# Five pairs of split weight tiles, four loaded ones, and seven-product sums that grow in two PSUM tiles

## The chip, the cores and the metric

The kernel runs on one NeuronCore of one Trainium2 chip. Times are device microseconds of one execution of the whole program; a time is the median of a few executions, and beside it stands the profile of one execution, whose span is a little shorter than its time. The engines are named as in the profile: PE (matrix multiplies; PEld are its weight loads), DVE (vector engine), ACT (scalar engine), POOL (GpSimd) and SP (issues DMAs).

## The reference

One decoder layer over 1024 prompt tokens and 8 sequences of 4 decode tokens, 1056 tokens in all, in float32. The parts that the change touches are the two FFN products into the hidden width of 2816:

```python
def _layer(x, p, ...):
    ...
    x = x + _rms(mix, n_mix_post)
    f = _rms(x, n_ffn_pre)
    f = (jax.nn.silu(f @ w_gate) * (f @ w_up)) @ w_down
    x = x + _rms(f, n_ffn_post)
    x = x + jax.nn.sigmoid(x @ w_ple_gate) * (p @ w_ple)
```

Before it stand an input projection, a causal pooling mixer, sliding-window attention with sinks, and an output projection.

## The kernel before

**Tiles.** Tokens lie along the free dimension in three groups of 352 (groups 0, 1 and 2), channels along the 128 partitions. Each float32 product is made of three reduced-precision ones: an operand is split into a rounded part and the rest (`split`, L163: ScalarE casts the rounded part, L164, VectorE subtracts it, L165), and `gemm` (L278) issues high x high, high x low and low x high for each 128 channels. A product over 512 channels is 12 matmuls of 128x352, one over 1024 channels 24.

**The FFN.** The hidden width is cut into 22 chunks of 128, two to a slab. `WALK` lists the order of slabs: entries 0 to 4 do slabs 0 to 4 for group 2 alone, entries 5 to 10 do slabs 5 to 10 for all three groups, entries 11 to 15 do slabs 0 to 4 for groups 0 and 1. `gate_up` does one chunk of one entry. Group 2 is multiplied directly (`direct`, 24 matmuls for gate and 24 for up). Groups 0 and 1, gate and up together, are a 2x2 block product that is done with seven 512-channel products instead of eight (`product`, 12 matmuls each): two use quarters of the gate tile (with `f7["B11"]`, `f7["B21"]`), one a quarter of the up tile (`T4`), and four use sums and differences of weight quarters, S1 to S4 (with `T1`, `T2`, `T3`, `B22`). The products are added to one another in SBUF on VectorE, read once each from PSUM (`add`, L1024).

**The weight sums.** `w_sums` (L980) makes S1 to S4 in place in the two loaded tiles: four POOL operations (L990), which can only begin when both loaded tiles have been split (the subtraction reads them), and then two casts (`sh`) and two subtractions (`sl`) of 128x1024.

**The down products.** `downs` of an entry are issued inside the first chunk of the next one (`pending`): 8 output tiles per group of 6 matmuls each, every one read from PSUM by VectorE and added to `os_` (L1087). The first of them that read a chunk's result wait for `hid_put` (L977), a cast on ScalarE and a subtraction on VectorE.

**Pools and order.** Split weights lie in 2 x `W_PAIRS` tiles, loaded ones in `W_RAW` tiles. PSUM has 8 banks, one tile each (`bank`). `need` makes the weight items up to `LOOK` = 4 ahead in the program. The order on PE is pinned to the program's order; on ScalarE, VectorE and POOL a scheduler sets it when the program is built, and each engine then runs its instructions in that order. VectorE and ScalarE work of the norms (`ple_steps`, `ffn_steps`) is dealt out between products by `turn`.

Of the kernel before, what the change touches and what calls it, by code (L numbers as in the profile page):

```python
# [12 lines left out]
AF = mybir.ActivationFunctionType  # L13
ALU = mybir.AluOpType
# [33 lines left out]
UEXT = PST + DSEQ  # L48
ULEN = UPRE + SEQ + NDEC * UEXT

W_PAIRS = 4
W_RAW = 3


WARM = 8
# [6 lines left out]
def trunk_kernel(  # L62
# [31 lines left out]
    nc = tc.nc  # L94
    te, ve, se, ge = nc.tensor, nc.vector, nc.scalar, nc.gpsimd
# [10 lines left out]
    def nm(s):  # L106
        cnt[0] += 1
        return f"{s}{cnt[0]}"
# [15 lines left out]
    def mm(*args, **kw):  # L124

        ins = te.matmul(*args, **kw)  # L126
# [63 lines left out]

    def weights(j, ahead=W_PAIRS - 1):
        for i in range(j, j + (0 if lazy[0] else ahead) + 1):
# [71 lines left out]
    def need(k, ahead=LOOK):  # L264

        for i in range(len(made), min(k + ahead + 1, len(ITEMS))):
            kind, js = ITEMS[i]
            if kind == "direct":
                w_split(js[0])
                made[i] = pairs[js[0]]  # L270
            else:
                made[i] = w_sums(*(raws[ITEMS[j][1][0]] for j in js))
            for kind, js in ITEMS[i + 1 : i + 3]:
                if kind == "direct":
                    w_load(js[0])
        return made[k]

    def gemm(ps, ops, start=True, stop=True):  # L278

        last = len(ops) - 1  # L280
        for i, (wh, wl, xh, xl) in enumerate(ops):
            mm(ps, wh, xh, start=start and i == 0, stop=False)
            mm(ps, wh, xl, start=False, stop=False)
            mm(ps, wl, xh, start=False, stop=stop and i == last)

    def ops8(w, xs):

# [147 lines left out]
    n = 4 * NDEC * PST  # L435
# [145 lines left out]
    for c in range(4):  # L581
        n = NDEC * DSEQ
# [356 lines left out]
    f7 = {}  # L939
# [37 lines left out]
    def hid_put(g, slot, ht):  # L977
        split(new_hid[g][:, slot, :], new_hid[g][:, SLAB + slot, :], ht)
# [20 lines left out]
    def ops4(w, x):  # L999

        return [(w[0][:, k, :], w[1][:, k, :], x[0][:, k, :], x[1][:, k, :]) for k in range(4)]

    def quarter(w, h):
        return tuple(t[:, 4 * h : 4 * h + 4, :] for t in w)

    def gate_up(items, slot, gs, pending):

        ig, iu, is_ = items
        n = N

        def product(w, x):
            ps = bank()
            gemm(ps[:, :n], ops4(w, x))
            turn(12)
            return ps[:, :n]

        def direct(w):
            ps = bank()
            gemm(ps[:, :n], ops8(w, fs[2]))
            turn(24)  # L1020
            return ps[:, :n]

        def add(out, a, ps):
            ve.tensor_tensor(out, a, ps, op=ALU.add)  # L1024

        wg = need(ig)
        if 0 in gs:
            p1 = tmp(n, "p1")
            se.copy(p1, product(quarter(wg, 0), f7["B11"]))
        if 2 in gs:  # L1030
            sl = tmp(n, "sl")
            se.activation(sl, direct(wg), AF.Silu)
        if 0 in gs:
            c11 = tmp(n, "c11")
            add(c11, p1, product(quarter(wg, 1), f7["B21"]))
            se.activation(c11, c11, AF.Silu)
        if pending and 0 in gs:
            pending()
        wu = need(iu)
        if 2 in gs:  # L1040
            ve.tensor_tensor(sl, sl, direct(wu), op=ALU.mult)
        for g in gs:
            if slot == 0:
                new_hid[g] = half(g, F32R, "hid")
        if 2 in gs:
            hid_put(2, slot, sl)
        if pending and 0 not in gs:
            pending()
        if 0 not in gs:
            return  # L1050
# [7 lines left out]
        if 2 in gs:  # L1058
# [8 lines left out]
        se.activation(p1, p1, AF.Silu)  # L1067
        ve.tensor_tensor(u3, u3, p1, op=ALU.mult)
        hid_put(1, slot, u3)

    os_ = [None] * G

# [204 lines left out]
```

## Time and profile before

| | before |
|---|---|
| median of 3 runs | 1118.25 us (1117.61 to 1118.88) |
| the profiled execution | 1118.37 us, its span 1116.6 us |
| PE busy | 1106.5 us (99%), 7171 matmuls |
| DVE busy | 748.3 us (67%) |
| ACT busy | 440.0 us (39%) |
| POOL busy | 179.4 us (16%) |
| mean granted PE clock | 0.998 |

Busy time is a share of the whole span. PE's matmuls are pipelined: one of 128x352 is shown with some 0.32 us, and they start some 0.16 us apart. The idle time named beside a group of instructions is that of its engine just before it, with what ended it. The entries of `WALK` that carry all three groups lie at about 400 to 770 us of the span, entries 11 to 15 at about 770 to 985 us.

### The profile page before, as it was taken

What the parts mean: (1) busy time and instruction counts of PE and PEld (TensorE: products, weight loads), DVE (VectorE), ACT (ScalarE), POOL (GpSimd) and SP (SyncE); (2) the same over time, 40 slices, a digit from 0 to 9 for tenths busy, and PEclk for the clock granted to TensorE, in tenths of its full rate; (3) what the DMA queues carried; (4) which work ended last, traced back from release to release, by engine and by line L of the source; (5) the groups of instructions that cost most, each with busy time, mean ns of one, the idle gap of its engine ahead of it and who ended that gap; (6) DMA issues with size and microseconds to landing.
All of it is one profiled execution on the core that took longest, in us unless ns stands there. A gap on an engine that the chain in (4) does not pass through costs nothing.

```text
span 1116.6 us, 17703 instructions
## 1 busy us (share of the span) xinstructions
PE 1106.5 (99%) x7171; PEld 1089.6 (98%) x7171; DVE 748.3 (67%) x1241; ACT 440.0 (39%) x779; POOL 179.4 (16%) x152
## 2 busy tenths in 40 slices
PE   8999999999999999999999999999999999999998
PEld 8999988899999999999999999999999999999998
DVE  6667478886979955255564555547887877789532
ACT  8323276664645523331222313123424334365220
POOL 0045032200000131011111102112132123100000
PEclk9999999999999999999999999999999999999999
DMA  8121311542543212121120202122112222336211
GB/s 289 56 71 38 122 43 38 194 157 85 203 166 129 99 38 76 39 76 39 38 60 17 78 36 76 38 100 79 57 58 83 70 76 80 124 133 222 85 58 39
DMA packets 35217, 99.54 MB, mean 89 GB/s; under 512 B 4132, under 2 KB 14660, under 8 KB 35136
## 3 DMA queue, kind: packets, MB, share of 16 engines
q1 hardware_dynamic: 33808, 96.65, 25.5%
q10 hardware_dynamic: 1328, 1.77, 0.5%
q8 instruction: 56, 0.92, 0.3%
q14 instruction: 25, 0.20, 0.1%
HBM read 88.30 MB, written 10.11 MB: 88 GB/s over the span
## 4 chain that ended last, share of the span: by engine, by line
PE 93%; DVE 3%; DMA 1%; issue 1%; POOL 1%; ACT 1%; SPq 0%; DVEq 0%; POOLq 0%
PE b L126 92%; PE b L120 1%; DMA xr<-in_x_dram 1%; DVE wl L165 1%; POOL wr L990 0%; SPq L342 0%; DVE h L368 0%; DVE o L1115 0%; DVE x L1119 0%; DVE mx L628 0%; DVE a L736 0%; DVE p L1024 0%; DVE hid L165 0%; ACT h L366 0%; ACT xr L377 0%
## 5 line engine op out<-in xcount | busy, mean ns | idle before, releaser
L126 PE MATMUL b<-fh,wh 128*128 128x352 f32 x808 | 260.7, 323 | 0.0
L126 PE MATMUL b<-fh,wl 128*128 128x352 f32 x808 | 259.3, 321 | 0.0
L126 PE MATMUL b<-fl,wh 128*128 128x352 f32 x808 | 259.0, 321 | 0.0
L126 PE MATMUL b<-hid,wh 128*128 128x352 f32 x1056 | 252.5, 322 | 1.8 <-DVE o L1115 1.2
L164 ACT CAST wh<-wr 128x1024 fp32r<-128x1024 f32 (+1 forms) x139 | 143.0, 1031 | 248.9 <-PE b L126 205.6
L165 DVE TENSOR_TENSOR wl<-wr,wh 128x1024 fp32r<-128x1024 f32 (+1 forms) x139 | 170.5, 1229 | 57.9 <-ACT wh L164 53.9
L126 PEld LDWEIGHTS b<-hid,wh 128*128 128x128 f32 x1056 | 182.3, 188 | 2.6 <-issue 1.5
L126 PE MATMUL b<-hid,wl 128*128 128x352 f32 x528 | 169.0, 320 | 0.0
L990 POOL TENSOR_TENSOR wr<-wr 128x512 f32<-128x512 f32 x44 | 63.4, 1441 | 623.0 <-DVE wl L165 621.3
L126 PEld LDWEIGHTS b<-fl,wh 128*128 128x128 f32 x808 | 151.9, 188 | 0.0
L126 PEld LDWEIGHTS b<-fh,wl 128*128 128x128 f32 x808 | 151.8, 188 | 0.0
L126 PEld LDWEIGHTS b<-fh,wh 128*128 128x128 f32 x808 | 151.6, 188 | 0.0
L1087 DVE TENSOR_TENSOR o<-o,b 128x352 f32<-128x352 f32 x240 | 114.9, 516 | 29.3 <-PE b L126 29.3
L126 PE MATMUL b<-fh,sh 128*128 128x352 f32 x352 | 113.6, 323 | 0.0
L126 PE MATMUL b<-fl,sh 128*128 128x352 f32 x352 | 112.7, 320 | 0.0
L126 PE MATMUL b<-fh,sl 128*128 128x352 f32 x352 | 112.7, 320 | 0.0
L126 PE MATMUL b<-h,wh 128*128 128x352 f32 x480 | 105.5, 325 | 0.9 <-ACT h L366 0.6
L165 DVE TENSOR_TENSOR sl<-wr,sh 128x1024 fp32r<-128x1024 f32 x44 | 53.8, 1222 | 75.5 <-ACT sh L164 75.5
L126 PEld LDWEIGHTS b<-hid,wl 128*128 128x128 f32 x528 | 98.9, 187 | 0.0
L164 ACT CAST sh<-wr 128x1024 fp32r<-128x1024 f32 x44 | 45.7, 1047 | 130.9 <-POOL wr L990 91.2
L126 PEld LDWEIGHTS b<-h,wh 128*128 128x128 f32 x480 | 81.9, 189 | 2.2 <-DVE h L368 1.2
L126 PE MATMUL b<-h,wl 128*128 128x352 f32 x240 | 66.3, 326 | 0.0
(150 smaller groups left out, 1591.0 us busy)
## 6 DMA issues: line engine op xcount, KB each, us to landing
wr<-in_w_gu_dram SPq DMA_DIRECT2D x64, 512.0 KB, 3.3
wr<-in_w_dn_dram SPq DMA_DIRECT2D x32, 512.0 KB, 3.3
wr<-in_w_pg_dram SPq DMA_DIRECT2D x14, 512.0 KB, 3.6
x<-in_x_dram SPq DMA_DIRECT2D x6, 704.0 KB, 7.1
x1d<-x SPq DMA_DIRECT2D x6, 704.0 KB, 3.5
x<-x1d SPq DMA_DIRECT2D x6, 704.0 KB, 6.7
out_y_dram<-yo SPq DMA_DIRECT2D x24, 176.0 KB, 1.9
wr<-in_w_out_b_dram SPq DMA_DIRECT2D x8, 512.0 KB, 3.3
```

Source lines behind the costliest of these rows:

```text
L120: ins = te.transpose(out, src, ident)
L126: ins = te.matmul(*args, **kw)
L164: fix(se.copy(hi, src))
L165: fix(ve.tensor_tensor(lo, src, hi.bitcast(F32), op=ALU.subtract))
L990: ge.tensor_tensor(out, a, b, op=op)
L1087: ve.tensor_tensor(o, o, v, op=ALU.add)
```

## The change

- `W_PAIRS` goes from 4 to 5 and `W_RAW` from 3 to 4: ten tiles of split weights instead of eight, four loaded ones instead of three. Room for them comes from a smaller scratch area that the program reserves for DMAs.
- Two PSUM tiles, `row` and `col`, take several of the seven products, one added to the other by PE (`start=False`, `onto=True`). `row` grows by B11, S2, S3 and, where group 2 takes part, T4; `col` by S1 and S4.
- Between the products a partial sum is read out. ScalarE copies it (`copied`: after B11, after S2, after S1 and, in the chunks without group 2, after S3), VectorE adds the rest. A product onto `row` or `col` may not begin before the copy of what it held.
- The order of products within a chunk changes. With group 2 it was B11, gate for group 2, B21, (downs), up for group 2, S2, S3, T4, S1, S4, and is now B11, gate for group 2, B21, (downs), S2, S1, S3, S4, up for group 2, T4. Without group 2 it was B11, B21, (downs), T4, S2, S3, S1, S4, and is now B11, B21, (downs), T4, S2, S1, S3, S4.

```diff
-W_PAIRS = 4
-W_RAW = 3
+W_PAIRS = 5
+W_RAW = 4
...
-    def gemm(ps, ops, start=True, stop=True):
+    def gemm(ps, ops, start=True, stop=True, onto=False):
...
-            mm(ps, wh, xh, start=start and i == 0, stop=False)
+            mm(ps, wh, xh, start=start and i == 0, stop=False, skip_group_check=onto)
...
-        def product(w, x):
-            ps = bank()
-            gemm(ps[:, :n], ops4(w, x))
+        def product(w, x, ps=None, start=True):
+            onto = ps is not None
+            ps = ps if onto else bank()
+            gemm(ps[:, :n], ops4(w, x), start, onto=onto)
             turn(12)
             return ps[:, :n]
...
-        def add(out, a, ps):
+        def add(a, ps, s):
+            out = tmp(n, s)
             ve.tensor_tensor(out, a, ps, op=ALU.add)
+            return out
+
+        def copied(ps, s):
+            out = tmp(n, s)
+            se.copy(out, ps)
+            return out
...
         if 0 in gs:
-            p1 = tmp(n, "p1")
-            se.copy(p1, product(quarter(wg, 0), f7["B11"]))
-        if 2 in gs:
+            row = bank()
+            p1 = copied(product(quarter(wg, 0), f7["B11"], row), "p1")
+        if third:
             sl = tmp(n, "sl")
             se.activation(sl, direct(wg), AF.Silu)
         if 0 in gs:
-            c11 = tmp(n, "c11")
-            add(c11, p1, product(quarter(wg, 1), f7["B21"]))
+            c11 = add(p1, product(quarter(wg, 1), f7["B21"]), "c11")
             se.activation(c11, c11, AF.Silu)
...
-        if 2 not in gs:
+        s = need(is_)
+        col = bank()
+        if not third:
             p4 = product(quarter(wu, 1), f7["T4"])
-        s = need(is_)
-        add(p1, p1, product(s["S2"], f7["T2"]))
-        u3 = tmp(n, "u3")
-        add(u3, p1, product(s["S3"], f7["T3"]))
-        c21 = tmp(n, "c21")
-        if 2 in gs:
-            p4 = product(quarter(wu, 1), f7["T4"])
-        add(c21, u3, p4)
-        ve.tensor_tensor(c21, c21, c11, op=ALU.mult)
-        hid_put(0, slot, c21)
-        p5 = product(s["S1"], f7["T1"])
-        add(u3, u3, p5)
-        add(p1, p1, p5)
-        add(p1, p1, product(s["S4"], f7["B22"]))
-        se.activation(p1, p1, AF.Silu)
-        ve.tensor_tensor(u3, u3, p1, op=ALU.mult)
-        hid_put(1, slot, u3)
+        u2 = copied(product(s["S2"], f7["T2"], row, False), "u2")
+        p5 = copied(product(s["S1"], f7["T1"], col), "p5")
+        p7 = product(s["S3"], f7["T3"], row, False)
+        if not third:
+            u3 = copied(p7, "u3")
+        u1 = add(p5, p7, "u1")
+        if not third:
+            ve.tensor_tensor(u3, u3, p4, op=ALU.add)
+            ve.tensor_tensor(u3, u3, c11, op=ALU.mult)
+            hid_put(0, slot, u3)
+        c12 = add(u2, product(s["S4"], f7["B22"], col, False), "c12")
+        se.activation(c12, c12, AF.Silu)
+        ve.tensor_tensor(u1, u1, c12, op=ALU.mult)
+        hid_put(1, slot, u1)
+        if third:
+            third_up()
+            ve.tensor_tensor(c11, c11, product(quarter(wu, 1), f7["T4"], row, False), op=ALU.mult)
+            hid_put(0, slot, c11)
...
-    nc = _bacc.Bacc("TRN2", target_bir_lowering=False, num_devices=1)
+    nc = _bacc.Bacc("TRN2", target_bir_lowering=False, num_devices=1, dynamic_dma_scratch_size=1024)
```

On PE the rows are as many as before (6129), and they differ only inside `gate_up`. On ACT they go from 667 to 721, on DVE from 1206 to 1122. Three places on ACT carry the prediction. Names end in a number that tells buffers of one kind apart: `wr` is a loaded weight tile, `wh` the rounded part of a direct tile, `sh` that of a summed one, `b` a PSUM tile, `hid` a hidden operand; `p`, `u`, `c` and `sl` are the sums of a chunk.

**First place**: ACT in the first chunk of entry 11 (slab 0, groups 0 and 1), from the casts of the weights of the second chunk on. Before:

```order
L164 CAST wh_7589<-wr_7462 128x1024
L164 CAST wh_7700<-wr_7556 128x1024
L304 ACT_TABLE_LOAD
L304 ACTIVATE sd_7874<-b_7869,c_86 88x4
L164 CAST sh_7818<-wr_7462 128x1024
L164 CAST hid_7828<-c_7900 128x352
L164 CAST sh_7822<-wr_7556 128x1024
L1029 COPY p_7944<-b_7945 128x352
```

Changed:

```order
L164 CAST wh_7652<-wr_7508 128x1024
L305 ACT_TABLE_LOAD
L305 ACTIVATE sd_7826<-b_7821,c_86 88x4
L164 CAST sh_7770<-wr_7390 128x1024
L1033 COPY u_7836<-b_7510 128x352
L1033 COPY p_7850<-b_7788 128x352
L164 CAST sh_7774<-wr_7508 128x1024
L1033 COPY u_7864<-b_7510 128x352
```

`b_7510` is this chunk's `row`, `b_7788` its `col`. The cast `sh_7770` is of the second chunk's sums, and the copy of `row` after S2 (`u_7836`) stands behind it. `wr_7508` is the second chunk's up tile: `wh_7652` takes over the buffer of the down weights that entry 11's `pending` uses last.

**Second place**: ACT in the first chunk of entry 12. Before:

```order
L164 CAST wh_8118<-wr_7996 128x1024
L164 CAST wh_8186<-wr_8083 128x1024
L164 CAST hid_8270<-c_8320 128x352
L164 CAST sh_8260<-wr_7996 128x1024
L164 CAST sh_8264<-wr_8083 128x1024
L1067 ACTIVATE p_8085<-p_8085 128x352
```

Changed:

```order
L164 CAST wh_8070<-wr_7935 128x1024
L164 CAST wh_8138<-wr_8035 128x1024
L1033 COPY u_8256<-b_8037 128x352
L164 CAST sh_8212<-wr_7935 128x1024
L1033 COPY p_8270<-b_8230 128x352
L164 CAST sh_8216<-wr_8035 128x1024
L1033 COPY u_8284<-b_8037 128x352
```

Here the copy of `row` after S2 stands ahead of the summed cast, and the copy of `col` after S1 (`p_8270`) behind it. Entries 13, 14 and 15 have the same sequence. In the first chunks of entries 5 to 10 both copies stand ahead of the summed casts.

**Third place**: ACT from the end of entry 11's second chunk into entry 12. Before:

```order
L164 CAST wh_7975<-wr_7847 128x1024
L164 CAST wh_7992<-wr_7942 128x1024
L1067 ACTIVATE p_7944<-p_7944 128x352
L1029 COPY p_8085<-b_8086 128x352
L164 CAST hid_7829<-u_8018 128x352
L164 CAST sh_8075<-wr_7704 128x1024
L1036 ACTIVATE c_8100<-c_8100 128x352
L164 CAST sh_8079<-wr_7942 128x1024
```

Changed:

```order
L164 CAST wh_7931<-wr_7894 128x1024
L1033 COPY u_7997<-b_7896 128x352
L164 CAST sh_8027<-wr_7656 128x1024
L1033 COPY p_8050<-b_8037 128x352
L1078 ACTIVATE c_8017<-c_8017 128x352
L164 CAST sh_8031<-wr_7894 128x1024
L164 CAST hid_7780<-u_7997 128x352
L164 CAST hid_7781<-u_7999 128x352
```

Both casts of hidden operands stood ahead of the summed casts or, for the first of the chunk, further up; now both stand behind `sh_8027` and `sh_8031`. On DVE the subtraction that belongs to `sh_8027` likewise stands ahead of those that belong to `hid_7780` and `hid_7781`. `wh_7931`, the next up tile, takes over a buffer that S3 of this second chunk uses last. In entries 13 to 15 the `hid` casts stand ahead of the `sh` casts.

More of the change, by code (lines that the diff above doesn't have):

```diff
@@ L276, in need @@
         return made[k]
-    def gemm(ps, ops, start=True, stop=True):
+    def gemm(ps, ops, start=True, stop=True, onto=False):
         last = len(ops) - 1
         for i, (wh, wl, xh, xl) in enumerate(ops):
-            mm(ps, wh, xh, start=start and i == 0, stop=False)
-            mm(ps, wh, xl, start=False, stop=False)
-            mm(ps, wl, xh, start=False, stop=stop and i == last)
+            mm(ps, wh, xh, start=start and i == 0, stop=False, skip_group_check=onto)
+            mm(ps, wh, xl, start=False, stop=False, skip_group_check=onto)
+            mm(ps, wl, xh, start=False, stop=stop and i == last, skip_group_check=onto)
     def ops8(w, xs):
@@ L1044, in gate_up, with third_up @@
                 new_hid[g] = half(g, F32R, "hid")
-        if 2 in gs:
+        def third_up():
+            ve.tensor_tensor(sl, sl, direct(wu), op=ALU.mult)
             hid_put(2, slot, sl)
-        if pending and 0 not in gs:
-            pending()
         if 0 not in gs:
+            third_up()
+            if pending:
+                pending()
             return
-        if 2 not in gs:
+        s = need(is_)
+        col = bank()
+        if not third:
             p4 = product(quarter(wu, 1), f7["T4"])
-        s = need(is_)
-        add(p1, p1, product(s["S2"], f7["T2"]))
-        u3 = tmp(n, "u3")
-        add(u3, p1, product(s["S3"], f7["T3"]))
-        c21 = tmp(n, "c21")
-        if 2 in gs:
-            p4 = product(quarter(wu, 1), f7["T4"])
-        add(c21, u3, p4)
-        ve.tensor_tensor(c21, c21, c11, op=ALU.mult)
-        hid_put(0, slot, c21)
-        p5 = product(s["S1"], f7["T1"])
-        add(u3, u3, p5)
-        add(p1, p1, p5)
-        add(p1, p1, product(s["S4"], f7["B22"]))
-        se.activation(p1, p1, AF.Silu)
-        ve.tensor_tensor(u3, u3, p1, op=ALU.mult)
-        hid_put(1, slot, u3)
+        u2 = copied(product(s["S2"], f7["T2"], row, False), "u2")
[13 more added lines that the diff above has]
+        if third:
+            third_up()
+            ve.tensor_tensor(c11, c11, product(quarter(wu, 1), f7["T4"], row, False), op=ALU.mult)
+            hid_put(0, slot, c11)
     os_ = [None] * G
```

2 lines of the change are left out of this document (1 added, 1 removed).

## The prediction

> **What bounds the kernel now.** I read the page's busy times first, then PE's waits, then the chain of waits. From the page, from the list of PE's waits (microseconds in total, times, longest) and from the chain:
>
> ```profile
> PE 1106.5 (99%) x7171; PEld 1089.6 (98%) x7171; DVE 748.3 (67%) x1241; ACT 440.0 (39%) x779; POOL 179.4 (16%) x152
> ...
> PE b L126 <- DVE acc L334: 1.3, 1, 1.3
> PE b L126 <- DVE o L1115: 1.2, 1, 1.2
> PE b L348 <- POOL c L147: 1.1, 1, 1.1
> PE b L126 <- ACT h L366: 0.6, 1, 0.6
> PE b L126 <- DVE hid L165: 0.6, 1, 0.6
> ...
> 862.35 1.23 DVE sl L165
> 863.58 1.54 DVE o L1115
> 865.25 131.54 PE b L126 x830
> ```
>
> PE is the bound: it idles 1116.6 - 1106.5 = 10.1 us in the whole span, and this is the most that shorter work elsewhere could give. Of its waits only two stand in the part that is changed: one for a hidden operand (`hid` L165, 0.6) and one for an eviction that came late behind a summed weight's subtraction (`o` L1115, 1.2; the chain shows it at 863 us). With their restarts I count 0.7 and 1.4 us, 2.1 together. The rest belongs to the start and the early stages. The last row gives PE's pace: 131.54 / 830 = 0.1585 us for a matmul, so a 12-matmul product takes 1.90 us, a down tile of 6 takes 0.95.
>
> **PE's own work** doesn't change: the matmuls are as many, in another order. An edit can move the end only by a wait of PE that it removes or makes.
>
> **Fewer adds, more copies.** From the groups by shape:
>
> ```profile
> L1024 DVE TENSOR_TENSOR p<-p,b 128x352 f32<-128x352 f32 x66 | 34.1, 516 | 6.1 <-PE b L126 5.5
> L1029 ACT COPY p<-b 128x352 f32<-128x352 f32 x22 | 9.7, 442 | 0.9 <-PE b L126 0.9
> ```
>
> Twelve chunks with group 2 lose 4 adds each and ten without it lose 3: 78 x 0.516 = 40 us of VectorE's 748. The first twelve gain 2 copies each, the ten 3: 54 x 0.442 = 24 us of ScalarE's 440. Both engines are busy for 67% and 39% beside PE's 99%, so as sums these are worth 0. If that cover were gone they would count in full, 24 against 40. What counts is where a copy stands, because PE now waits for it: a product onto `row` or `col` can't start before it.
>
> **Wider pools.** No wait of PE's names a DMA or a weight cast, so a buffer more on either side buys 0. The extra loads that run ahead add no bytes. It could cost something only if a split moved in front of work that PE waits for; the orders show no such case in the FFN but those below.
>
> **Where the copies stand.** ScalarE runs its list in order, and 22 times it stands still behind POOL's weight sums. PE has until now waited for nothing queued there. The list of ScalarE's waits, and rows of the timeline of entry 11 (start, duration, engine, line, idle time before and its releaser; the first two rows are PE's last down matmul and the next product's first):
>
> ```profile
> ACT sh L164 <- POOL wr L990: 91.2, 22, 6.3
> ...
> 784.29 0.32 PE L126 MATMUL b<-hid,wl 128*128 128x352 f32 x1
> 784.45 0.32 PE L126 MATMUL b<-fh,wh 128*128 128x352 f32 x1
> 784.49 1.05 ACT L164 CAST wh<-wr 128x1024 fp32r<-128x1024 f32 x1 [5.84 <-PE b L126]
> 786.40 1.05 ACT L164 CAST wh<-wr 128x1024 fp32r<-128x1024 f32 x1 [0.86 <-PE b L126]
> 787.48 1.23 DVE L165 TENSOR_TENSOR wl<-wr,wh 128x1024 fp32r<-128x1024 f32 x1 [0.68 <-ACT wh L164]
> 788.27 0.71 PE L126 MATMUL b<-c,acc 128*88 128x1 f32 x8
> 788.84 1.28 POOL L990 TENSOR_TENSOR wr<-wr 128x512 f32<-128x512 f32 x1 [20.73 <-DVE wl L165]
> 790.20 2.82 POOL L990 TENSOR_TENSOR wr<-wr,wr 128x512 f32<-128x512 f32 x2
> 793.09 1.46 POOL L990 TENSOR_TENSOR wr<-wr 128x512 f32<-128x512 f32 x1
> 794.58 1.05 ACT L164 CAST sh<-wr 128x1024 fp32r<-128x1024 f32 x1 [5.30 <-POOL wr L990]
> ```
>
> Cast, subtraction, four sums, summed cast: from 786.40 to 795.63, 9.23 us. A cast that waits for the end of the downs starts 0.04 us after PE's next product (784.49 - 784.45). Call that moment T0. In the changed order the last `wh` cast ahead of the sums waits for exactly that in the first chunk of entries 11 to 15, so the first `sh` cast ends at T0 + 9.27, a copy behind it at 9.27 + 0.44 = 9.71, and PE has it at 9.8 (0.1 for the handing over, as from 788.71 to 788.84 above).
>
> - **A**, entry 11 (first order above). S3 goes onto `row` and needs `u_7836`, which stands behind `sh_7770`. Until then PE has T4, S2 and S1, 36 x 0.1585 = 5.71 us, and the norm's small matmuls, 788.84 - 788.27 = 0.57. Stall: 9.8 - 6.28 = **3.5 us**.
> - **B**, entries 12 to 15 (second order). S4 goes onto `col` and needs `p_8270`, behind `sh_8212`; PE has four products, 7.61 us. Stall 2.2 us, four times: **8.8 us**.
> - **C**, entry 12's downs (third order). `wh_7931` starts at the end of S3 of entry 11's second chunk. From there `sh_8027` ends at 9.27; behind it a copy, a Silu, `sh_8031` and the first `hid` cast:
>
> ```profile
> L1067 ACT ACTIVATE p<-p 128x352 f32<-128x352 f32 x22 | 10.9, 496 | 20.2 <-DVE p L1024 20.2
> L164 ACT CAST hid<-u 128x352 fp32r<-128x352 f32 x22 | 10.7, 485 | 8.1 <-DVE u L1068 7.8
> L165 DVE TENSOR_TENSOR hid<-u,hid 128x352 fp32r<-128x352 f32 x22 | 13.9, 632 | 4.4 <-ACT hid L164 4.4
> ```
>
>   9.27 + 0.44 + 0.50 + 1.05 + 0.49 = 11.75, and VectorE's subtraction, 0.52 to 0.63, brings 12.3. PE has S4, B11 and B21, 5.71, and the four matmuls of the first down tile that read the older half, 0.63. Stall: 12.3 - 6.34 = **5.95 us**. It takes the place of the 0.7 above.
> - **D**, entry 13's downs, and then 14's and 15's. Here the `hid` casts stand ahead, and what comes late are evictions on VectorE behind `sl`, as in the second wait above:
>
> ```profile
> 862.35 1.23 DVE L165 TENSOR_TENSOR sl<-wr,sh 128x1024 fp32r<-128x1024 f32 x1 [3.71 <-ACT sh L164]
> ```
>
>   VectorE stands 3.71 us before it, and PE runs out of PSUM banks. `row` and `col` hold two banks now, so I take some more than the 1.4 of before: 1.75, and 0.15 for each of the two later ones: **2.05 us**. Its bounds are 0 and 2 x 1.4 = 2.8.
>
> In the first chunks of entries 5 to 10 both copies stand ahead of the `sh` casts, so each is over 0.44 us after its product, and another product of 1.90 us lies between it and the one that needs it. The hidden operands of group 0 now come last in a chunk, but before the first down tile PE has B11, group 2's gate and B21 of the next one, 48 x 0.1585 = 7.6 us, and then group 2's four tiles. I cost these at 0; if that cover were gone, a cast and a subtraction (0.5 + 0.6) in six chunks would cost 6.6 us.
>
> Sum: 3.5 + 8.8 + 5.95 + 2.05 - 2.1 = +18.2, on the profiled execution's 1118.37: **1136.6** (it lies 0.1 above the median). The unknown in A to C is the 9.23: VectorE's part may wait for an eviction (0.52), a hand-over may take 0.1 more or less, so I take plus or minus 0.7 for each of the six stalls, some 4 us in all.
>
> **The clock.** Windows at the start of the span (from:to, us, busy time and count of PE, PEld, DVE, ACT, POOL, then PE's granted clock):
>
> ```profile
> 21.96:25.38 3.42, 2.08 (x17) 1.79 (x16) 3.42 (x7) 3.42 (x7) 0.00 (x0) 1.00 0.73 226
> 25.38:28.79 3.41, 3.23 (x12) 2.72 (x11) 3.38 (x9) 2.54 (x5) 0.86 (x2) 0.50 0.02 6
> 28.79:32.20 3.41, 3.41 (x23) 3.41 (x22) 3.41 (x7) 3.30 (x8) 0.00 (x0) 1.00 0.00 0
> ```
>
> A window in which PE was busy for 61% is followed by one at half the clock, worth 3.41 x 0.5 = 1.7 us. The wait at 863 (1.4 us) has no such window behind it; the mean clock of the whole span is 0.998. Six stalls of 2.2 to 6 us can each be followed by one: 0 to 10.2 us. I take three (A, C and one of B's): 3 x 1.7 = +5.1, **1141.7**. Its own range is that of the stalls and of one window fewer or more: some 1137 to 1146.
>
> The Trainium skill ("TensorE: Matmul & The Clock Gate", section "Why this matters for your kernels") asks one to avoid gaps of PE longer than about 3 us, since the clock may halve after them. The trace differs: the window ahead of the half-clock one holds 3.42 - 2.08 = 1.3 us of idle time in all. By the page's rule alone only A and C would pay, 1136.6 + 3.4 = 1140.0; by the row each stall might, 1136.6 + 10.2 = 1146.8.
>
> **The rivals.**
> - *The stalls, but no clock cut* (0.17): **1136.6**. For it: the 863 wait has none behind it. Against it: A and C are longer than any wait of PE's in the list above.
> - *All six pay a half-clock window* (0.12): **1146.8**. For it: the windows above. Against it: B's stalls are not much longer than the 863 wait.
> - *PSUM banks rather than copies* (0.05): the copies come in time, since the weight buffers come free before the end of the downs, but with two banks held every one of the ten down groups of entries 11 to 15 has a wait like that of 863: 10 x 1.4 - 2.1 = +11.9, **1130.3**. For it: the wait at 863 is of this kind, with a bank fewer. Against it: the orders' casts wait for the last down matmuls.
> - *Not slower* (0.11): the casts find their buffers free early (the fifth pair), POOL's sums are over before PE is through with its products, and the two old waits vanish: **1116.3**. Its point of decision is the `sh` cast ending more than 3.5 us sooner in A. A gain here is at most those 2.1 us, and more only if some of PE's 8 us of idle time at the start went too, so most of it (0.07) is no difference and 0.04 a gain. Against it: in the profile of before, the same chain starts at the end of the downs.
>
> **How the numbers follow.** The forecast, stalls with some half-clock windows, has 0.55 and gives 1141.7. The range leaves out the not-slower rival (0.11), half of the bank rival and the outer ends of the others: from the bank rival's 1130.3, and 1136.6 less the 4 of the stalls, to 1131 below; above, 1146.8 and half of the 4: 1149. What a measurement can tell from no change is about 0.2%, 2.2 us. Slower by more than that: 0.55 + 0.17 + 0.12 + 0.05 = 0.89; within it 0.07; faster 0.04.
>
> **What would show it.** In the profile of the changed kernel: PE's waits name ScalarE's copies (`u`, once some 3.5 us, for A; `p`, four times some 2.2, for B) and one `hid` of some 6 us (C); PE's gaps lie in 785 to 990 us of the span, with windows of clock 0.5 behind some; ahead of 770 us PE has no new wait; VectorE's busy time is about 708 (748 - 40), ScalarE's about 464 (440 + 24). Wrong would be: PE waits that name the copies of entries 5 to 10, gaps that start anywhere but behind T4 to S4, a first `sh` cast in entries 11 to 15 that ends less than 8 us after the downs, or a time under 1130.

## The result

| | before | changed |
|---|---|---|
| median | 1117.93 us (4 runs, 1117.0 to 1118.88) | 1137.1 us (4 runs, 1135.96 to 1138.48) |
| profiled execution, its span | 1118.37, 1116.6 us | 1137.5, 1135.7 us |
| mean granted PE clock | 0.998 | 0.993 |

The changed kernel takes 1.0174 times as long (95% interval 1.0159 to 1.0189): 19 us more. The forecast was 1141.7, with a range from 1131 to 1149.

### The profile page after: what moved, and what is told of

The parts are those of the page before. It is cut to its first block, busy times and chain, and to the rows that moved or that the text cites. A ratio compares the mean times of both kernels' runs of the same rounds, so it can differ in the third digit from the quotient of the medians.

```text
span 1135.7 us, 17639 instructions
## 1 busy us (share of the span) xinstructions
PE 1112.1 (98%) x7171; PEld 1093.9 (96%) x7171; DVE 723.3 (64%) x1163; ACT 462.6 (41%) x833; POOL 182.3 (16%) x152
## 3 DMA queue, kind: packets, MB, share of 16 engines
q1 hardware_dynamic: 33808, 96.65, 25.2%
## 4 chain that ended last, share of the span: by engine, by line
PE 41%; issue 36%; POOL 11%; DMA 5%; DVE 3%; ACT 2%; SPq 0%; POOLq 0%; ACTq 0%; DVEq 0%
PE b L126 40%; POOL wr L991 11%; DMA wr<-in_w_gu_dram 4%; DVE sl L165 2%; ACT sh L164 1%; PE b L120 1%; DMA xr<-in_x_dram 1%; DMA a<-in_dmask_dram 1%; SPq L343 0%; DVE h L369 0%; DVE mx L629 0%; DVE a L737 0%; DVE c L1028 0%; DVE wl L165 0%; ACT wh L164 0%
## 5 line engine op out<-in xcount | busy, mean ns | idle before, releaser
L126 PE MATMUL b<-hid,wh 128*128 128x352 f32 x1056 | 255.3, 324 | 7.0 <-ACT hid L164 5.0
L165 DVE TENSOR_TENSOR wl<-wr,wh 128x1024 fp32r<-128x1024 f32 (+1 forms) x139 | 170.0, 1224 | 84.6 <-ACT wh L164 72.2
L991 POOL TENSOR_TENSOR wr<-wr 128x512 f32<-128x512 f32 x44 | 60.3, 1371 | 639.3 <-DVE wl L165 637.6
L1102 DVE TENSOR_TENSOR o<-o,b 128x352 f32<-128x352 f32 x240 | 117.5, 516 | 45.0 <-PE b L126 44.9
L165 DVE TENSOR_TENSOR sl<-wr,sh 128x1024 fp32r<-128x1024 f32 x44 | 53.6, 1223 | 70.0 <-ACT sh L164 69.6
L126 PEld LDWEIGHTS b<-fh,sh 128*128 128x128 f32 x352 | 66.6, 189 | 10.5 <-ACT p L1033 7.3
```

Of the source, the lines that this page charges most:

```text
L165: fix(ve.tensor_tensor(lo, src, hi.bitcast(F32), op=ALU.subtract))
L991: ge.tensor_tensor(out, a, b, op=op)
L1102: ve.tensor_tensor(o, o, v, op=ALU.add)
```

## The profile after, beside the one before

The page's busy times, and the first four rows of the list of PE's waits (us in total, times, longest), of the changed kernel:

```profile
PE 1112.1 (98%) x7171; PEld 1093.9 (96%) x7171; DVE 723.3 (64%) x1163; ACT 462.6 (41%) x833; POOL 182.3 (16%) x152
...
PE b L126 <- ACT p L1033: 6.1, 4, 1.6
PE b L126 <- ACT hid L164: 5.0, 1, 5.0
PE b L126 <- ACT u L1033: 2.9, 1, 2.9
PE b L126 <- DVE hid L165: 2.0, 3, 0.7
```

PE does the same 7171 matmuls. The waits on a copy `p` (four times), a cast `hid` (once), a copy `u` (once) and a subtraction `hid` (three times) are new; the two of the kernel before, on `hid` L165 and `o` L1115, are gone. Of the other rows, all from outside the FFN, one of 1.3 us at the start (`acc`) is gone, and three grew by 0.2 to 0.4 us each.

**A**, rows of the timeline of entry 11 (here and below some rows between are left out; start, duration, engine, line, idle time before and its releaser):

```profile
783.15 1.05 ACT L164 CAST wh<-wr 128x1024 fp32r<-128x1024 f32 x1 [6.35 <-PE b L126]
784.23 1.23 DVE L165 TENSOR_TENSOR wl<-wr,wh 128x1024 fp32r<-128x1024 f32 x1 [0.40 <-ACT wh L164]
785.54 1.29 POOL L991 TENSOR_TENSOR wr<-wr 128x512 f32<-128x512 f32 x1 [26.47 <-DVE wl L165]
...
791.16 1.04 ACT L164 CAST sh<-wr 128x1024 fp32r<-128x1024 f32 x1 [3.22 <-POOL wr L991]
792.11 0.45 ACT L1033 COPY u<-b 128x352 f32<-128x352 f32 x1
792.61 0.43 PE L126 MATMUL b<-fh,sh 128*128 128x352 f32 x1 [2.93 <-ACT u L1033]
```

The chain is the one that was forecast, link by link: a cast at the end of the downs, subtraction, sums, summed cast, copy, and PE's S3 at 792.61. The start of PE's previous matmul is 789.37, so PE stood for 792.61 - 789.37 - 0.159 = 3.1 us. From the cast's start to the end of the summed cast it took 792.20 - 783.15 = 9.05 us (9.23 before). The copy begins 0.09 us before the cast ahead of it has ended, so it adds less than its own duration.

**B**, entry 12 (entries 13 to 15 look the same):

```profile
846.82 1.04 ACT L164 CAST sh<-wr 128x1024 fp32r<-128x1024 f32 x1 [3.38 <-POOL wr L991]
847.77 0.45 ACT L1033 COPY p<-b 128x352 f32<-128x352 f32 x1
848.27 0.43 PE L126 MATMUL b<-fh,sh 128*128 128x352 f32 x1 [1.50 <-ACT p L1033]
```

PE's matmul before started at 846.44: 1.67 us of standing. The four are 1.67, 1.79, 1.67 and 1.67.

**C**, at the head of entry 12's downs:

```profile
814.12 2.78 DVE L1134 SCALAR_TENSOR_TENSOR x<-o,c,x 128x352 f32<-128x352 f32 x2
817.68 0.72 DVE L1075 TENSOR_TENSOR u<-u,c 128x352 f32<-128x352 f32 x1
818.05 1.04 ACT L164 CAST sh<-wr 128x1024 fp32r<-128x1024 f32 x1 [6.72 <-POOL wr L991]
819.00 0.45 ACT L1033 COPY p<-b 128x352 f32<-128x352 f32 x1
819.35 0.50 ACT L1078 ACTIVATE c<-c 128x352 f32<-128x352 f32 x1
819.74 1.03 ACT L164 CAST sh<-wr 128x1024 fp32r<-128x1024 f32 x1
820.68 0.87 ACT L164 CAST hid<-u 128x352 fp32r<-128x352 f32 x2
821.22 1.22 PE L126 MATMUL b<-hid,wh 128*128 128x352 f32 x2 [4.96 <-ACT hid L164]
```

The matmul before started at 815.93; PE stood for 5.1 us. The queue of ScalarE is the forecast one: summed cast, copy, Silu, second summed cast, `hid`. The first two rows are VectorE's: two steps of group 2's norm, 2.78 us, and then the `u` that the `hid` cast reads.

**D**, entry 13's downs, and here the forecast named the wrong thing:

```profile
865.52 2.98 POOL L991 TENSOR_TENSOR wr<-wr,wr 128x512 f32<-128x512 f32 x2
867.28 3.12 DVE L165 TENSOR_TENSOR hid<-u,hid 128x352 fp32r<-128x352 f32 x2
868.58 1.44 POOL L991 TENSOR_TENSOR wr<-wr 128x512 f32<-128x512 f32 x1
868.94 0.43 PE L126 MATMUL b<-hid,wh 128*128 128x352 f32 x1 [0.69 <-DVE hid L165]
```

PE waits for no eviction but for the subtraction of a hidden operand, and the row of two takes 3.12 us, some 1.6 each, where its like takes 0.52. POOL is at its sums nearly the whole time, to 870.02. Three such waits cost 0.86, 0.79 and 0.86 us.

The clock, in windows behind the waits A, C and B (from:to, us, busy time and count of PE, PEld, DVE, ACT, POOL, granted clock):

```profile
793.64:797.05 3.41, 3.41 (x15) 3.41 (x14) 0.08 (x1) 1.16 (x2) 0.00 (x0) 0.59 0.51 159
820.92:824.33 3.41, 3.12 (x10) 2.85 (x11) 3.13 (x6) 0.63 (x2) 0.00 (x0) 0.50 0.63 186
824.33:827.74 3.41, 3.41 (x15) 3.41 (x14) 1.78 (x5) 0.50 (x1) 0.00 (x0) 0.58 0.33 126
850.23:853.64 3.41, 3.41 (x24) 3.41 (x23) 3.17 (x7) 2.04 (x4) 0.00 (x0) 1.00 0.86 262
```

One window at half the clock follows A (3.1 us), two follow C (5.1 us), none follows a B (1.7 us). The entries with all three groups show nothing: between 380 and 760 us PE is busy for all 380 us in both kernels, with as many matmuls:

```profile
380.00:760.00 380.00, 380.00 (x2394) 380.00 (x2393) 191.80 (x286) 120.33 (x189) 74.38 (x52) 1.00 0.17 56
```

**The account**, from the starts of PE's matmuls in the two traces. The new waits are 3.1 + 6.8 + 5.1 + 2.5 = 17.5, the old ones 2.1, so 15.4 more; the half clock takes 5.1; and what lies ahead of the FFN came out 1.3 us shorter: 15.4 + 5.1 - 1.3 = 19.2 us, against 1135.7 - 1116.6 = 19.1 in the spans.

## The experiments

Each kernel stands beside the kernel before in its own comparison; the ratio is to that.

**The pools alone.**

```diff
-W_PAIRS = 4
-W_RAW = 3
+W_PAIRS = 5
+W_RAW = 4
```

> The kernel before with five pairs and four loaded tiles, its seven products as they were. Theory (the wider pools buy nothing, since PE waited for no load and no split; the time comes from copies that PE waits for): PE's waits list stays as before, within 1.5 us of it, 1117 to 1119.5. In the first downs of entry 12 the second group's hid cast now stands behind the first summed cast, which may cost up to 1 us. Rival (the wider pools are at fault, by transfers or splits that collide): 1125 or more.

Measured: 1124.19 us, 1.0051 (1.0038 to 1.0064). Neither: 6.3 us slower than before, with no product changed. The list of PE's waits and the timeline of entry 13:

```profile
PE b L126 <- DVE c L1024: 2.7, 1, 2.7
PE b L126 <- DVE o L1087: 1.7, 1, 1.7
```

```profile
859.83 1.99 ACT L164 CAST sh<-wr 128x1024 fp32r<-128x1024 f32 x2 [3.56 <-POOL wr L990]
860.92 2.36 DVE L165 TENSOR_TENSOR sl<-wr,sh 128x1024 fp32r<-128x1024 f32 x2 [3.64 <-ACT sh L164]
863.19 0.51 DVE L1024 TENSOR_TENSOR c<-p,b 128x352 f32<-128x352 f32 x1
```

With another tile free, both summed subtractions stand ahead of everything that empties PSUM banks on VectorE; with four pairs it was one of the two. VectorE stands for 3.64 us and then does both, and PE, out of banks, stands for 2.9 us at 860.7 and, for an eviction too, 1.9 at 909, with one half-clock window behind the longer. A third wait, 1.15 us at 815, is for a hidden subtraction. None of the three names a transfer. By the starts of PE's matmuls these waits are 3.8 us more than before and the window some 1.6; what is left of the 5.5 us in the spans is a start that is 1.3 us shorter and some 1.5 us in the distance between PE's matmuls, of which more below. So most of what the pools cost came through the order that the scheduler makes of them.

**The new products with the old pools.** The changed kernel with `W_PAIRS = 4`, `W_RAW = 3`.

> The changed products with the four pairs and three loaded tiles of before. Here the scheduler puts both copies ahead of the summed cast in the first chunks of entries 11 to 15, and of the two hid casts only the second behind the first summed cast. Theory (a stall is made by a copy's place on ScalarE, not by summing in PSUM): stalls A and B vanish; in four or five entries the second hid operand comes at 9.27 + 0.44 + 0.50 + 0.5 + 0.6 = 11.3 us after the third product where PE is at 5.7 + 3.8 + 0.6 = 10.1, so 1.2 us each: 1121 to 1124, with no half-clock window in the FFN. Rival (sums in PSUM cost PE by themselves, by banks or by waits for any copy): 1132 or more.

Measured: 1140.56 us, 1.0196 (1.0182 to 1.021). The forecast failed, though what it said of the copies held: A and all four Bs shrank to between nothing and 0.85 us. The time went into the hidden operands. PE's waits, and the timeline at the head of entry 12's downs:

```profile
PE b L126 <- DVE hid L165: 7.0, 6, 3.6
PE b L126 <- ACT hid L164: 5.2, 4, 1.6
```

```profile
813.17 3.10 POOL L991 TENSOR_TENSOR wr<-wr,wr 128x512 f32<-128x512 f32 x2
813.55 3.10 DVE L1134 SCALAR_TENSOR_TENSOR x<-o,c,x 128x352 f32<-128x352 f32 x2
816.57 1.58 DVE L165 TENSOR_TENSOR hid<-u,hid 128x352 fp32r<-128x352 f32 x1
```

I had read the order on ScalarE and not the one on VectorE: two steps of group 2's norm stand ahead of the subtraction, and all three instructions are slow beside POOL, 1.55, 1.55 and 1.58 us where 0.66 and 0.52 are usual. The wait there is 3.8 us. In three later slabs two waits of 1.7 and 1.15 us follow each other within 2 us, and each pair has a half-clock window behind it.

**The new products in the chunks with group 2 only.** The seven products of the kernel before wherever group 2 is not in the chunk; the pools stay wide.

> The changed kernel with the old products in the chunks without group 2, the new ones in the twelve chunks with group 2. Theory: nothing of the new products costs anything in the chunks with group 2, so A, B, C and their half-clock windows vanish: 1117 to 1119.5, no gap of PE between 375 and 770 us. Rival (the new products cost or save something in every chunk): outside that range.

Measured: 1124.71 us, 1.0056 (1.0042 to 1.0069). A, B and C are gone, and the time is that of the pools alone, with waits in the same three places (1.15, 3.35 and 1.4 us). So the new products cost nothing and give nothing in the twelve chunks with group 2; all their harm is in the ten others.

**The copies first.** `copied` keeps its instruction, the second chunk's sums are asked for behind the last copy of the first, and the casts of the sums are queued behind the copies and the hidden casts:

```diff
-        wu = need(iu)
+        wu = need(iu, 3 if few else LOOK)
...
-        s = need(is_)
+        s = need(is_, 2 if few else LOOK)
...
+        if few:
+            behind[:] = [last_copy[0]]
+            need(is_)
...
+                for ins in behind:
+                    stack.enter_context(tc.issue_after(ins.ins))
                 split(*hl, src)
```

(`few`: the first chunk of a slab without group 2.)

> The changed kernel, computing the same, with the summed casts queued behind the chunk's copies and hidden casts on ScalarE (and the subtractions that belong to them on VectorE): in the first chunks without group 2 the second chunk's sums are asked for after the copies, and all summed casts there are queued behind. Theory: A, B, C and the half-clock windows vanish, 1137.5 - 3.1 - 6.8 - 5.1 - 4.6 = 1117.9; the three waits of 0.7 to 0.9 us for a hid subtraction stay, and one more may take C's place: 1117 to 1120. Rival (it is the two held banks, or PSUM sums as such): 1130 or more. Rival (the summed weights now come too late for the next chunk): a new wait of PE for sl, 1120 to 1130.

Measured: 1124.65 us, 1.0057 (1.0045 to 1.007). 12.5 us of the 19 are gone, and none of the Bs is left, so the place of the copies was the cause of A and B, and the held banks were not. It stays above the forecast by 5:

```profile
PE b L126 <- ACT hid L164: 2.7, 1, 2.7
PE b L126 <- DVE hid L166: 2.5, 4, 0.7
PE b L126 <- ACT p L1040: 1.2, 1, 1.2
```

The first is in C's place: 2.9 us and a half-clock window. There the hidden operand waits for VectorE, which does the norm's `x<-o,c,x` beside POOL's sums (2.77 us for two). The changed kernel has the same chain beneath C, hidden by the longer one on ScalarE (the rows of C above: `u` is ready at 818.40, and PE's wait begins at 816.1). The last is a copy behind a weight cast and a table load. The three waits of D stayed as they were, 0.87 us each.

**One sum more.**

```diff
-            (a12, a12, a11, ALU.subtract),
+            (a12, a12, a11, ALU.subtract), (a12, a12, a11, ALU.subtract),
```

> The changed kernel with the last of POOL's four weight sums done twice, the order of ScalarE and VectorE unchanged. (S1 is then another matrix than it should be; every instruction and its size stay.) Theory (PE waits for a copy, and that for the sums): a sum takes 1.35 us, so A, C and the four Bs grow by 1.35 each, 6 x 1.35 = 8.1 in all: A 4.4, B 3.0 to 3.1, C 6.5. The Bs of 1.7 had no half-clock window behind them, the other kernels' waits of 2.9 had one: with one behind each B, 4 x 1.7 = 6.8 more, 1137.1 + 8.1 + 6.8 = 1152, and up to 4 more if D grows with the sums: 1150 to 1156. If the clock doesn't follow, 1145 to 1149. Rival (the waits don't hang on the sums): 1137 to 1140.

Measured: 1162.18 us, 1.0391 (1.0375 to 1.0407).

```profile
PE b L126 <- ACT p L1033: 11.2, 4, 2.9
PE b L126 <- ACT hid L164: 6.4, 1, 6.4
PE b L126 <- ACT u L1033: 4.4, 1, 4.4
```

From the starts of PE's matmuls, A went from 3.1 to 4.5, C from 5.1 to 6.5, the Bs from 1.7 to 3.0, 3.1, 2.9 and 2.9: each longer by 1.2 to 1.5, one sum. That the waits hang on POOL's sums is shown. And each B has now a half-clock window behind it, where none had:

```profile
855.80:859.90 4.10, 1.26 (x8) 0.97 (x7) 1.23 (x1) 2.33 (x4) 1.65 (x2) 0.99 0.00 0
859.90:863.30 3.40, 3.40 (x14) 3.40 (x13) 2.34 (x4) 1.41 (x3) 0.00 (x0) 0.51 0.64 175
```

The time is above the forecast by 6 us and more. By the trace the waits brought 9.3 us over the changed kernel, the clock some 9 (A, C and one of the Bs have two windows each), and 6.3 us came from a thing that no theory had: PE's matmuls started 161.1 ns apart instead of 158.9, from 398 us of the span on to the wait C at 830, and again in parts behind it.

**The sums after the hidden operand.** The kernel with the copies first, and POOL's sums in a slab's second chunk behind a small copy that reads the last hidden subtraction:

```diff
+    seen = const([P, 1], dt=F32R)
...
+                token[:] = [ge.tensor_copy(seen, new_hid[1][:, SLAB + slot, 0:1])]
```

> The kernel with the copies first, computing the same; in the second chunk of a slab without group 2, POOL's sums wait in addition for the last subtraction of the hidden operands (a copy of 128x1 on POOL that reads it stands ahead of them). Theory (VectorE's instructions that read two operands from SBUF take 1.5 us instead of 0.5 beside POOL's sums, and this makes the three waits of 0.86 and lengthens the one at 813): the three waits vanish (2.6), the one of 2.9 + 0.6 shrinks to 1.5 or less and loses its half-clock window (1.7): 1117.5 to 1120. Rival (the waits come from VectorE's order, not from POOL): no change, 1124 to 1125.5. Rival (the sums, 2 us later, now hold back the subtractions of the summed weights and the evictions behind them): new waits for o, 1120 to 1127.

Measured: 1129.29 us, 1.0099 (1.0086 to 1.0113): the third theory, and 2 us above its range. (The profiled execution took 1126.89 us, the shortest of the four.) The three waits of D are gone, as the first theory said, and the wait at 813 shrank from 2.9 to 0.9 us with its half-clock window gone. But the sums are later now, VectorE stands longer before `sl`, and the evictions behind it are late: PE has two waits for `o`, by the starts of its matmuls 2.15 and 2.21 us. So D came from POOL's work beside VectorE, and delaying POOL alone moves the wait to the evictions.

**The sums late, in both kernels.** Both repairs together: POOL's sums behind the hidden operand, and the summed weights of the next slab asked for in the middle of the downs, so that the first `sl` stands behind more of the evictions (three to eight in the traces):

```diff
-        wg = need(ig)
+        wg = need(ig, 3 if later else LOOK)
...
-        wh, wl = need(WD[n][m // 4], 0 if n == len(WALK) - 1 else LOOK)
+        wh, wl = need(WD[n][m // 4], 0 if n == len(WALK) - 1 else 2 if few else LOOK)
```

(`later` and `few`: the next slab is one without group 2, and `m < 4`.) In the kernel before:

> The kernel before, computing the same, with two edits and its own pools and products: the summed weights of the next slab's first chunk are asked for in the middle of the downs, so that their subtractions stand behind the first evictions on VectorE; and POOL's sums there wait for the last subtraction of the hidden operands. Theory: the two waits of the FFN, 0.73 and 1.38 us, vanish, and nothing else is there to gain: 1117.9 - 2.1 = 1115.8, 1115 to 1117. Rival (the sums come too late for S2 then): 1118 or more, with PE waiting for sl.

In the changed kernel, with the copies first:

> The changed kernel's products and pools, computing the same, with everything that was found: copies ahead of the summed casts, the sums asked for in the middle of the downs, and POOL's sums behind the last hidden subtraction. Theory (the new products cost PE nothing by themselves; what they cost is the place of the copies): what is left is the wait of 1.35 at 799 for a copy behind a weight cast and a table load, and up to 1.5 at 813; 1117 to 1119.5, within 0.2% of before. Rival (two PSUM tiles held over several products, or ScalarE's reads, cost PE in every slab): above 1121.

Measured: 1119.41 us, 1.0015 (1.0006 to 1.0024), and 1122.28 us, 1.0042 (1.003 to 1.0055). Both above the forecast, although the waits did what was expected: the kernel before has no wait in the FFN any more, and the changed one has four, of 1.35, 0.9, 0.6 and 0.6 us. What grew was again the distance between PE's matmuls, 160.0 ns instead of 158.9 from 350 us of the span on. It cost 2.8 us in each up to 750 us; behind that the kernel before kept it, for some 1.1 us more, and the changed one fell back to 158.9 at the wait at 818. All three kernels with the constant `seen` had it. That made the next test.

**The constant alone.** The kernel before with

```diff
+    seen = const([P, 1], dt=F32R)
+    ge.tensor_copy(seen, ones[:, 0:1])
```

> The kernel before with one more constant of 128x1 (four bytes in each partition), which POOL fills once and nobody reads. Theory (PE's rhythm, 158.9 or 160.0 ns a matmul, goes with where things lie in SBUF: all three kernels with this constant ran at 160.0): 160.0 in the FFN, 3 to 4.5 us more, 1120.5 to 1122.5. Rival (the rhythm comes from the order of instructions or is chance): 158.9 in the FFN, 1117 to 1118.5.

Measured: 1122.51 us, 1.0037 (1.0024 to 1.0049), at the upper end of what the first theory said: 4.6 us slower for four bytes that nobody reads. In the profiled execution the distance accounts for 2.8 of 4.8 us; 1.9 were lost ahead of the FFN, where two windows at half the clock follow each other (25.6 to 32.4 us) and the kernel before has one. Two of the other executions, with a granted clock of 1.0, took 1120.95 and 1121.56 us, 3.0 and 3.6 more than the kernel before, so the part that goes with the distance is nearer to 3 us. Windows of 100 us in the same stretch, PE busy throughout and at full clock, of the kernel before and of this one; the count in the first brackets is that of matmuls:

```profile
500.00:600.00 100.00, 100.00 (x632) 100.00 (x631) 55.55 (x95) 22.98 (x34) 15.95 (x12) 1.00 0.15 48
```

```profile
500.00:600.00 100.00, 100.00 (x627) 100.00 (x626) 57.08 (x97) 23.15 (x34) 16.02 (x12) 1.00 0.16 53
```

These are 632 and 627 matmuls of one shape in the same time, and 623 in the kernel with a sum more, none of them waiting for anything that the profile shows.

**The two late kernels without the new constant** (the small copy writes to an unused column of an old one, `seen = ones[:, 5:6]`), and the kernel before with wide pools and the same repairs:

> The kernel before with late sums, with the two edits as they were, but POOL's small copy writes to a place of an old constant, so that no new one is allotted. Theory (places set the rhythm): 158.9 in the FFN, the two waits gone, 1115 to 1116.5, faster than before by 0.1 to 0.25%. Rival (the edits themselves change the rhythm): 160.0 and 1118.5 to 1120.

> The changed kernel's products and pools with all three repairs, no new constant. Theory: PE's rhythm at 158.9 in the FFN, so 3 us less than with the constant, 1118.5 to 1120 (the waits of 1.35, 0.9 and 0.6 us at 799 to 817 stay). Rival: the rhythm stays at 160.0, 1121.5 to 1123.

> The kernel before with five pairs and four loaded tiles, and the same two edits (sums asked for in the middle of the downs, POOL's sums behind the last hidden subtraction), no new constant. Theory (the 6.3 us of the wider pools alone come from both sl subtractions standing ahead of the evictions on VectorE, not from the pools): the waits of 1.2, 2.9 and 1.9 us and the half-clock window vanish: 1124.2 - 1.2 - 2.9 - 1.9 - 1.5 = 1116.7, 1115 to 1118 if PE's rhythm stays at 158.9. Rival (the pools cost something else too): 1120 or more.

Measured: 1114.67 us, 0.9972 (0.9962 to 0.9983); 1119.74 us, 1.0018 (1.0008 to 1.0027); 1120.35 us, 1.0019 (1.001 to 1.0027).

The first is the fastest of all, and faster than the kernel before. Its list of PE's waits has four rows left, none of the FFN's products or downs. By the starts of PE's matmuls it gains 2.5 us in the FFN, 2.1 of them the two waits, 0.7 ahead of the FFN and 0.9 by the closer distance, 158.9 also in the last stage, where the kernel before has 160.0.

The second came inside its range. Its distance is 158.9 in the entries with three groups, as forecast, but 161.1 in those with two, in a profiled execution that was the slowest of the eleven (1121.64); so the constant is not the only thing that sets it. The third took the time of its rival, 1120 or more, in part by the mechanism that it was to remove: in the last two slabs, whose order I had not read, `sl` stands behind two evictions only. At the first of them VectorE waits 5.41 us for the summed cast, and PE for 1.95, with a half-clock window:

```profile
907.18 1.23 DVE L165 TENSOR_TENSOR sl<-wr,sh 128x1024 fp32r<-128x1024 f32 x1 [5.41 <-ACT sh L164]
```

Another wait of 0.9 us is for a hidden subtraction, and 161.1 ns between 826 and 898 us took some 1.0 us; whether the pools have to do with that is open.

## Why the prediction was right, and where it was not

**The direction and the size** came from the right place: PE bound, nothing to gain but its few waits, and an in-order engine on which PE newly depends. The reading "ScalarE stands 22 times behind the sums, and PE has until now waited for nothing queued there" is the whole of the loss in A and B. In C it sets the length of the wait, but only 2.2 of the 5.1 us hang on it alone. Lengthening the sums by one lengthened all six waits by one sum; putting the copies ahead of the summed casts removed A and the Bs, and left 2.9 us in C's place. The measured 1137.1 lies closer to the rival without clock cuts (1136.6) than to the forecast 1141.7, but not by that rival's mechanism: the three half-clock windows came, while the waits brought 15.4 us instead of 18.2 and the start 1.3 less.

**A, B and C** were each forecast too long: 3.5 for 3.1, 8.8 for 6.8, 5.95 for 5.1. The chain itself was 0.1 to 0.4 us shorter than the 9.23 of before (8.84 to 9.16), and instructions that follow each other on ScalarE overlap by some 0.1 each, where the sum laid them end to end. In C the forecast also took the hidden operand's `u` as ready. It was not: VectorE finished it at 818.40, 2.3 us into the wait, behind two norm steps that were slow beside POOL. The forecast for C was near because the queue on ScalarE was longer still.

**D** had about the right size (2.05 for 2.5) by luck, and the wrong cause. It was not the evictions behind `sl` that came late but the hidden operand's subtraction, three times as long as its row in the profile of before, because POOL's sums ran beside it. The rows were there to be read, in the groups by shape and in the chain of the kernel before:

```profile
L1119 DVE SCALAR_TENSOR_TENSOR x<-o,c,x 128x352 f32<-128x352 f32 x24 | 15.3, 664 | 0.0
L165 DVE TENSOR_TENSOR hid<-sl,hid 128x352 fp32r<-128x352 f32 x22 | 11.5, 521 | 7.2 <-ACT hid L164 7.2
```

```profile
812.87 3.06 DVE x L1119 x2
815.93 1.53 DVE hid L165
```

Two norm steps of 1.53 us each where the mean is 0.66, and a hidden subtraction of 1.53 where the other kind has 0.52.

**The clock**: three windows were taken, and three came, 5.1 us. That the count was right is luck: one was given to a B, and it was C that had two. The mechanisms of the rival with no clock cut and of the one with six both failed in the trace.

**Wider pools at 0** is the step that failed. "No wait of PE's names a DMA" was true and did not answer the question: the pools change the order on VectorE, and by themselves they cost 6.3 us, most of it through that order. In the sum it did no harm, since A to D were read from the changed order, which had the pools in it. Nor do the two halves add up: the pools alone cost 6.3, the products alone 22.6, both 19.2, since each makes an order of its own.

**Adds and copies** were rightly taken as nothing. ScalarE's busy time came out as forecast (462.6 for 464), VectorE's did not (723.3 for 708): the sum of its durations fell by 31 us and not by 40, in the main because the new multiplications and subtractions read two operands from SBUF and are long beside POOL (`u<-u,c` 610 ns on average, `hid<-u,hid` 810); and its busy time fell by 25 only, as fewer of its instructions overlap.

**The start**: 1.3 us less ahead of the FFN was in no step. All nine kernels with wide pools have 0.8 to 1.3 us less there than the kernel before, the four others with narrow ones from 0.7 less to 2.0 more; whether the pools do it is left open. Some 0.8 of it in the profiled executions is there by 39 us: the kernel before has a half-clock window at 25.4 to 28.8, where PE has work in hand, the changed one at 8.0 to 11.4, where it costs little in the end, since both start their 126th matmul at 25.2 and 25.5 us. The prediction also put PE's 8 us of idle time outside the FFN at the start; the trace of before has 3.5 us of it in the first 30 us and 4.2 behind PE's last matmul.

With everything repaired the new products stand at 1.0018 of before and the old ones at 0.9972. This does not compare the products alone: the first has the wide pools, waits of 3.6 us and a distance of 161.1 in its last entries. With wide pools and the same repairs the old products stand at 1.0019, the same as the new ones. That the new products by themselves are worth about nothing is shown for the chunks with group 2; for the others it is argued from PE's unchanged count of matmuls, since no kernel ran them without waits.

## What to carry to other kernels

Before a read from PSUM is put on an engine so that the tensor engine has to wait for it, list what stands ahead of it on that engine, and price what the longest of these waits for, not the read. A wider pool is a change of order too: where a scheduler places instructions, read the new order on every engine that PE waits for, one slab after the other to the last, and not only on the engine that the edit names. And before a difference of half a per cent is put down to an edit, compare the distance between PE's matmuls in both traces, in a stretch where PE waits for nothing.

## What the runs showed of the hardware

**VectorE beside POOL.** While POOL does its sums, VectorE's instructions with two operands in SBUF take up to 1.6 us instead of 0.52, and those with one operand in PSUM stay at 0.51. Rows of the new products with the old pools:

```profile
861.28 1.46 POOL L991 TENSOR_TENSOR wr<-wr 128x512 f32<-128x512 f32 x1 [16.94 <-DVE wl L165]
862.14 0.98 DVE L165 TENSOR_TENSOR hid<-u,hid 128x352 fp32r<-128x352 f32 x1
862.81 2.98 POOL L991 TENSOR_TENSOR wr<-wr,wr 128x512 f32<-128x512 f32 x2
864.56 0.51 DVE L1028 TENSOR_TENSOR c<-p,b 128x352 f32<-128x352 f32 x1
```

The subtraction begins inside the first sum and ends at 863.12, 0.38 us after the sum has ended at 862.74. This holds throughout: in the fourteen traces 213 VectorE instructions of 128x352 with two operands in SBUF began with more than 0.2 us of a sum still to run, and every one ended 0.38 to 0.39 us after the end of that sum. The 506 with an operand in PSUM that began inside a sum took 0.50 to 0.53. In the kernel with POOL held back the same subtraction takes 0.53. The Trainium skill says it ("GPSIMD Engine Reference", section "1. Specifications"): POOL shares its access to SBUF with VectorE, and VectorE's instructions with two SBUF inputs are among those that collide. The trace agrees, and adds the price: what is left of POOL's sum, of 1.3 to 1.5 us, and 0.38 us.

**The clock behind a wait.** All twelve waits of PE of 2.88 us or more after the start had a window of some 3.4 us at half the clock behind them; C in the changed kernel and, with one sum more, A, C and a B (4.5, 6.5 and 3.1 us) had two. Of the single waits from 1.3 to 2.21 us one had a window behind it (1.95 us), the other fifteen had none, the one of 2.21 among them; three pairs of 1.7 and 1.15 us close together had one each. The Trainium skill's 3 us ("TensorE: Matmul & The Clock Gate", section "Why this matters for your kernels") is about right here as a rule for single waits, a little high.

**PE's distance between matmuls.** With no wait and at full clock, 128x352 matmuls start 158.9, 160.0 or 161.1 ns apart on average, and a kernel can keep one of these for hundreds of microseconds. Over the FFN that came to as much as 6 us, more than most of the edits here. In the profiled execution of each kernel the stretch with three groups had 160.0 in the four kernels with a new constant of four bytes in each partition, 158.9 in nine without it, and 161.1 in the one with a sum more, which changed over at 398 us without any wait of PE. In the entries with two groups the distance often changes at a wait: in the changed kernel it goes from 158.9 to 161.1 at the B of 893 us and back at the wait at 914, and in the kernel with the constant alone from 160.0 to 158.9 at the wait at 822. Why, no run here shows.
